# Two transformer blocks on one core: the seams between stages reordered, and memory attention's logits from query parts

## The chip, the cores and the metric

The kernel runs on one core of a Trainium2 chip. The engines are TensorE (PE), which multiplies matrices into PSUM, VectorE (DVE), ScalarE (ACT), GpSimd (POOL) and SyncE (SP), which here only issues transfers. Each engine works its instructions off in the order in which the program gives them. The metric is the device time of one execution in microseconds.

## The reference

Two blocks follow one another on 1024 rows of 1024 channels, all in float32. The first mixes three branches by gates, projects, and runs a gated MLP; the second has spatial gating, attention in a window and attention to 256 memory rows. Cut to what the change touches:

```python
def hybrid_layer(h, ...):
    ...
    y_b = attn @ w_b
    ...
    m = g[:, :, 0] * y_a + g[:, :, 1] * y_b + g[:, :, 2] * y_c
    h = h + m @ w_o
    hn = rms_norm(h, norm2_g)
    gate, up = jnp.split(hn @ w_gate_up, 2, axis=-1)
    return h + (jax.nn.silu(gate) * up) @ w_down

def memory_cross_attention(q, mem_k, mem_v):
    logits = jnp.einsum('bshd,bmhd->bhsm', q, mem_k).astype(jnp.float32) * (dh ** -0.5)
    probs = jax.nn.softmax(logits, axis=-1)
    out = jnp.einsum('bhsm,bmhd->bshd', probs.astype(mem_v.dtype), mem_v)
    return out.reshape(b, s, h * dh)

def second_block(x, mem, ...):
    h = rms_norm_2(x, pre_norm_g)
    a_u, a_v, sq, sk, sv, mq, z = jnp.split(h @ w_in, split_at, axis=-1)
    y_a = chunked_spatial_gating(jax.nn.gelu(a_u), jax.nn.gelu(a_v), ...)
    y_b = sliding_window_attention(sq, sk, sv, sinks, rel_bias)
    mk, mv = jnp.split(rms_norm_2(mem, mem_norm_g) @ w_mem_kv, 2, axis=-1)
    y_c = memory_cross_attention(mq, mk, mv)
    y = jnp.concatenate([y_a, y_b, y_c], axis=-1) * jax.nn.silu(z)
    return x + rms_norm_2(y @ w_out, post_norm_g)
```

Memory attention has 4 heads of 64 channels, so a query of one head fills half of the 128 rows that a product contracts.

## The kernel before

**Products in parts.** A float32 operand is split into a high part, rounded to fp32r, and a low part, the remainder. A product of two float32 matrices is then three fp32r products into one PSUM bank, high by high, high by low, low by high: `mm3`, lines L296 to L298, called from `proj_t` (weights as the stationary operand) and `proj_r` and `rows512` (rows as the stationary operand).

**Weights.** The class `Weights` walks a list (`plan`) of units of 128x1024 elements in the order in which the stages use them. `load_to` issues a unit's transfer on SP (L84) into one of three buffers (wraw), `split_to` makes the high part on ACT (L96) and the low part by a subtraction (L97) on POOL or DVE; the parts (wpart) have eight buffers. `get` hands units to a stage. `ahead_to(i)` splits the units up to i beyond those in use, and alternates between DVE and POOL for the low part; `ahead()` splits two ahead with POOL. Where the program calls them decides behind what these instructions stand in each engine's queue.

**Order.** The order on every engine is that in which the program's text issues the instructions. Stages follow one another: wb (the attention branch and the gated sum m), wo, the memory keys and values (mkv), the MLP (gate and up, then down), z, a (two halves: v with a layer norm, u), spatial gating, the heads' projections (qkv), attention (att2), and the last projection w2. At each seam the first weight units of the next stage must be split while the last tiles of this one are evicted. Side work runs on credits: a `Side` gets so many microseconds by each `tick` in PE's loops, times a rate, and issues its next step when it has credit. In wb two of them run: the normalisation and transposition of the 256 memory rows (`mem_steps`, scale L1090, transposes L1096, copies L1101 and L1102), and the expansion of the window's bias.

**wb.** For each of four weight pairs, two halves of the rows and two column tiles, PE fills a tile; DVE multiplies it by a gate (L1130) and adds the other branches' sum (L1131), both loaded by POOL (L1114 and L1115) one tile ahead; ACT writes the high part mh (L1132), POOL the low part ml (L358).

**wo to MLP.** `add_rows` adds a tile to the residual (L1303), takes the sum of squares and stores the row half (L1227, on SP). `norm2_b` norms a row block. The second half of wo is a loop of its own over the row blocks, with the norms and the splits for mkv between the tiles. `t1_sum`, `t2_sum` and `t3_sum` (L1239, L1566, L1243) form the sums of row blocks for the MLP's products; gate and up are computed with seven products of halves in place of eight. `gu_load`, `gu_sums` and `gu_prep` load, add and split the weights for one of them (L1265, L1272 to L1274, L1297 and L358), and `gu_mm(n, turns)` issues product n with the listed transposes between its matmuls: `turn4`, four transposes on PE (L1207) into a bank called ax, evicted by ACT (L1210) and DVE (L1211).

**rows512.** It fills eight row tiles from four weight units. The last two run unit by unit, and one tile's eviction is held back to behind them; then the next stage's units are split, and the last tiles are evicted by `put`. For the v half of stage a, `put` runs a layer norm by steps on DVE and POOL (L1803, L1804), so that an eviction brings POOL two products that wait for DVE.

**Attention.** Sixteen items, one of the window and one of memory for each row block, go through four stages: logits (L1933, PE; maxima on DVE), exps (ACT), turn (transposes L1969 of the probabilities and their copies), values (L1991). PE's queue interleaves stages of neighbouring items. The memory logits are one fp32 matmul 128x256 a head, whose queries mqp are zero in the other head's 64 rows.

## Time and profile before

| | |
|---|---|
| runs: median (lowest to highest) | 2199.52 us (2195.73 to 2200.37), 3 runs |
| the profiled execution | 2198.24 us |
| its span | 2196.5 us |
| its mean granted clock | 0.992 of full speed |

The span is what the trace covers, from the first instruction to the last; 1.74 us of the execution lie outside. The granted clock is TensorE's, 1.00 for 2.4 GHz and 0.50 for 1.2 GHz. Busy shares of the engines are means over stages that differ much: stages with products keep PE full, and what the other engines do is seen by PE only where it waits for them.

### The profile page before, as it was taken

How to read it: one execution, taken by the hardware profiler on the slowest of the kernel's cores; microseconds unless marked ns; L12 is line 12 of the kernel's file. 1: busy time of each engine (PE TensorE's matmuls, PEld its weight loads, DVE VectorE, ACT ScalarE, POOL GpSimd, SP SyncE). 2: the span in 40 equal slices, each digit the busy share in tenths (PEclk: the TensorE clock that was granted, in tenths of full speed). 3: DMA queues.
4: the chain of work that ended last, by engine and by line, in shares of the span. 5: the costliest groups of instructions: out<-in, count | busy, mean ns of one | idle time of the engine just before them, and what ended most of it. 6: DMA issues, size and time to landing. Idle time of an engine off the chain costs nothing.

```text
span 2196.5 us, 28194 instructions
## 1 busy us (share of the span) xinstructions
PE 2130.6 (97%) x10319; PEld 1796.9 (82%) x10319; DVE 1394.0 (63%) x2720; ACT 776.1 (35%) x1476; POOL 773.4 (35%) x675
## 2 busy tenths in 40 slices
PE   7999999999999999989989999999999999999998
PEld 7788888998888898777777888888788778778986
DVE  7688899889886587642765544454776651822725
ACT  4574211112112676332243333333433342212621
POOL 1213323225452320571048777785300001551201
PEclk9999999999999999999999999999999999999999
DMA  4121122112331000355213434334898422110014
GB/s 150 64 71 63 58 77 97 39 58 77 106 106 39 21 1 10 101 142 176 99 47 103 154 105 139 116 124 143 313 387 298 164 90 86 39 48 30 1 48 154
DMA packets 141227, 227.64 MB, mean 104 GB/s; under 512 B 15148, under 2 KB 77328, under 8 KB 141088
## 3 DMA queue, kind: packets, MB, share of 16 engines
q1 hardware_dynamic: 124544, 181.43, 24.6%
q0 software_dynamic: 9408, 30.15, 4.4%
q10 hardware_dynamic: 7136, 14.25, 1.7%
q8 instruction: 81, 1.33, 0.2%
q14 instruction: 58, 0.48, 0.1%
HBM read 170.46 MB, written 55.31 MB: 103 GB/s over the span
## 4 chain that ended last, share of the span: by engine, by line
PE 81%; DVE 7%; issue 4%; POOL 3%; DMA 3%; ACT 2%; SPq 0%; ACTq 0%; DVEq 0%; POOLq 0%
PE mm L297 23%; PE mm L298 23%; PE mm L296 23%; PE ax L296 2%; PE ax L297 2%; PE ax L298 2%; PE mm L1002 1%; PE ax L1991 1%; PE mm L1933 1%; POOL wpart L97 1%; PE mm L383 1%; DVE scores L611 1%; DMA ev<-mpart 1%; PE mm L1969 1%; DVE rt L287 1%
## 5 line engine op out<-in xcount | busy, mean ns | idle before, releaser
L97 POOL TENSOR_TENSOR wpart<-wraw,wpart 128x1024 fp32r<-128x1024 f32 (+1 forms) x88 | 211.4, 2416 | 726.6 <-ACT wpart L96 726.5
L297 PE MATMUL mm<-xl,wpart 128*128 128x512 f32 (+2 forms) x736 | 269.9, 367 | 0.0
L296 PE MATMUL mm<-xh,wpart 128*128 128x512 f32 (+2 forms) x736 | 268.9, 365 | 0.0
L298 PE MATMUL mm<-xh,wpart 128*128 128x512 f32 (+2 forms) x736 | 268.6, 365 | 0.0
L654 DVE MAX8 m<-scores 128x8 f32<-128x272 f32 (+6 forms) x224 | 188.8, 843 | 6.3 <-POOL scores L616 0.2
L656 DVE MATCH_REPLACE8 scores<-m,scores 128x272 f32<-128x272 f32 (+6 forms) x224 | 184.9, 826 | 0.0
L296 PE MATMUL mm<-tm,wpart 128*128 128x512 f32 x440 | 172.3, 392 | 1.3 <-DVE hb L1386 1.3
L298 PE MATMUL mm<-tm,wpart 128*128 128x512 f32 x440 | 171.4, 390 | 0.0
L297 PE MATMUL mm<-tm,wpart 128*128 128x512 f32 x440 | 171.3, 389 | 0.0
L96 ACT ACTIVATE wpart<-wraw 128x1024 fp32r<-128x1024 f32 (+1 forms) x110 | 112.7, 1049 | 161.2 <-issue 95.2
L358 POOL TENSOR_TENSOR wpart<-hb,wpart 128x512 fp32r<-128x512 f32 x88 | 118.8, 1357 | 135.9 <-ACT wpart L1297 135.9
L296 PEld LDWEIGHTS mm<-xh,wpart 128*128 128x128 f32 x736 | 138.4, 188 | 20.3
L297 PEld LDWEIGHTS mm<-xl,wpart 128*128 128x128 f32 x736 | 138.2, 188 | 19.7
L298 PEld LDWEIGHTS mm<-xh,wpart 128*128 128x128 f32 x736 | 138.5, 188 | 19.1
L297 PE MATMUL mm<-wpart,hh 128*128 128x512 f32 x256 | 101.9, 398 | 6.6 <-POOL wpart L97 3.6
L296 PE MATMUL mm<-wpart,hh 128*128 128x512 f32 x256 | 101.4, 396 | 0.0
L298 PE MATMUL mm<-wpart,hl 128*128 128x512 f32 x256 | 101.3, 396 | 0.0
L97 DVE TENSOR_TENSOR wpart<-wraw,wpart 128x1024 fp32r<-128x1024 f32 (+1 forms) x22 | 28.6, 1309 | 110.4 <-ACT wpart L96 110.3
L296 PEld LDWEIGHTS mm<-tm,wpart 128*128 128x128 f32 x440 | 82.6, 188 | 18.7 <-DVE hb L1386 1.7
L298 PEld LDWEIGHTS mm<-tm,wpart 128*128 128x128 f32 x440 | 82.6, 188 | 17.5 <-POOL wpart L358 0.2
L1297 ACT ACTIVATE wpart<-hb 128x512 fp32r<-128x512 f32 x88 | 55.0, 627 | 117.7 <-DVE hb L1290 60.1
L297 PEld LDWEIGHTS mm<-tm,wpart 128*128 128x128 f32 x440 | 82.7, 188 | 16.7
(388 smaller groups left out, 5393.0 us busy)
## 6 DMA issues: line engine op xcount, KB each, us to landing
wraw<-in_w_in_dram SPq DMA_DIRECT2D x68, 512.0 KB, 3.6
hd<-hb SPq DMA_DIRECT2D x100, 256.0 KB, 2.4
tm<-in_w_down_dram SPq DMA_DIRECT2D x99, 256.0 KB, 5.3
wraw<-in_w_gate_up_dram SPq DMA_DIRECT2D x44, 512.0 KB, 3.7
tm<-hd SPq DMA_DIRECT2D x33, 512.0 KB, 7.2
wraw<-hd SPq DMA_DIRECT2D x33, 256.0 KB, 5.3
mpart<-ev POOLq DMA_DIRECT2D x32, 256.0 KB, 2.3
ev<-mpart POOLq DMA_DIRECT2D x32, 256.0 KB, 3.4
```

The lines of the kernel that those rows point to most:

```text
L96: nc.scalar.activation(hi[:, :nk * w], r, AF.Copy)
L97: (low or nc.gpsimd).tensor_tensor(lo[:, :nk * w], r, hi[:, :nk * w].bitcast(F32), op=ALU.subtract)
L287: nc.vector.scalar_tensor_tensor(t, y, v, y, op0=ALU.mult, op1=ALU.mult)
L296: nc.tensor.matmul(o, sh, mh, start=start, stop=False, skip_group_check=more)
L297: nc.tensor.matmul(o, sh, ml, start=False, stop=False, skip_group_check=more)
L298: nc.tensor.matmul(o, sl, mh, start=False, stop=stop, skip_group_check=more)
L358: (eng or nc.gpsimd).tensor_tensor(out_lo, src, hi.bitcast(F32), op=ALU.subtract)
L383: nc.tensor.transpose(tp[:, k * 128:k * 128 + P], r[:, kk * 128:(kk + 1) * 128], ident[:P, :P])
L611: nc.vector.scalar_tensor_tensor(s, r, c["wr"][:, h:h + 1], s, op0=ALU.mult, op1=ALU.add)
L654: nc.vector.max(m8, s)
L656: nc.vector.match_replace(out=s, in_to_replace=m8, in_values=s, imm_value=TAKEN)
L1297: nc.scalar.activation(hi, src, AF.Copy)
```

## The change

The first part moves instructions at the seams and leaves the arithmetic alone: `rows512` splits the next units before the held eviction; wb's loop splits the last units before the last tile's eviction; the memory side work has a rate of 1.25; the work around the memory keys' products and the MLP's first products is issued in another order, with the transposes one product later; the low parts of z's third and fourth units go to DVE, each behind two row blocks' transposes; spatial gating goes over row halves outside and groups inside. A small tile for the sinks is shared with another.

The second part concerns memory attention. The 128 contracted rows now hold the high part of a head's queries in one half and the low part in the other (mqp, fp32r, by `put_parts`: two half copies on ACT, two subtractions on DVE, two transfers between row halves on POOL's queue, for each of four tiles). The keys stand in both halves, split into mkh and mkl. A head's logits are two fp32r products 128x256, with mkh and with mkl, in place of one fp32 product. The memory queries are projected first among the heads, and the clearing of mqp is dropped.

```diff
@@ -219,6 +219,6 @@
         plan_wide("a", w_in2, 512 * j)
+    plan_cols("s", w_in2, 256 * 6)
     for k0 in (0, 4):
         plan.append(("s", [cols(w_in2, 1024 + 64 * hd, 64, k0) for hd in (0, 2, 1, 3)], 4, 256))
-    for j in (5, 6):
-        plan_cols("s", w_in2, 256 * j)
+    plan_cols("s", w_in2, 256 * 5)
     for j in range(2):
@@ -350,4 +350,4 @@
         W.load_to(W.nu + 4)
-        put(held, order[-3])
         W.ahead_to(nxt)
+        put(held, order[-3])
         put(os_[0], order[-2])
@@ -1105,3 +1105,3 @@
 
-    memside = Side(mem_steps(), 1.1)
+    memside = Side(mem_steps(), 1.25)
     biasside = Side(bias_steps())
@@ -1120,3 +1120,6 @@
         units = W.get("wb", 2)
-        W.ahead()
+        if j < 3:
+            W.ahead()
+        else:
+            W.ahead_to(2)
         for t0, n in HALVES:
@@ -1129,2 +1132,4 @@
                 proj_t(o, units, ct * 128, oh, ol, 0, n)
+                if f == 7 and t0:
+                    W.ahead_to(4)
                 nc.vector.tensor_tensor(g, o, g, op=ALU.mult)
@@ -1133,3 +1138,2 @@
                 lo_of(ml[:, f, t0:t0 + n], p, mh[:, f, t0:t0 + n])
-    W.ahead_to(4)
     close(aop)
@@ -1142,5 +1146,2 @@
         gu_load(0)
-        norm2_b(7)
-        t1_sum(2)
-        t1_sum(3)
         e = ev()
@@ -1156,8 +1157,8 @@
         gu_prep(0, nc.vector)
+        norm2_b(7)
+        t1_sum(2)
+        t1_sum(3)
+        gu_prep(1, nc.vector)
         gu_sums(0)
         gu_load(1)
-        gu_prep(1, nc.vector)
-        for t in range(4):
-            t3_sum(t)
-        gu_prep(2, nc.vector)
         e = ev()
@@ -1171,3 +1172,3 @@
         nc.scalar.dma_start(mkd[1], e)
-        gu_prep(3, nc.vector)
+        gu_prep(2, nc.vector)
 
@@ -1321,2 +1322,4 @@
         proj_r(o, mh, ml, t * 128, wo, 0, 512)
+        if t == 7:
+            W.split_to(W.nu + 2, nc.vector)
         if t:
@@ -1327,4 +1330,2 @@
             t1_sum(t - 5)
-        if t == 7:
-            W.split_to(W.nu + 2, nc.vector)
         add_rows(1)(o, t)
@@ -1571,17 +1572,19 @@
 
-    gu_mm(0, [(5, 0), (5, 1), (5, 2)])
-    gu_prep(4)
+    gu_mm(0)
     gu_out(0)
-    gu_mm(1, [(7, 0), (7, 1), (7, 2)])
-    gu_prep(5)
-    gu_mm(2, [(5, 3), (3, 0), (3, 1)])
+    gu_mm(1, [(5, 0), (5, 1), (5, 2)])
+    for t in range(4):
+        t3_sum(t)
+    gu_prep(3)
+    gu_prep(4)
+    gu_mm(2, [(5, 3), (7, 0), (7, 1)])
     gu_out(2)
-    gu_mm(3, [(7, 3), (3, 2)])
-    for t in range(3):
-        t2_sum(t)
+    gu_prep(5)
+    gu_mm(3, [(7, 2), (7, 3), (3, 0)])
     gu_sums(1)
     gu_prep(6)
-    gu_mm(4, [(3, 3), (6, 0)])
-    t2_sum(3)
     gu_out(1)
+    gu_mm(4, [(3, 1), (3, 2), (3, 3)])
+    for t in range(4):
+        t2_sum(t)
     gu_out(3)
@@ -1589,3 +1592,3 @@
     gu_prep(7)
-    gu_mm(5, [(6, 1), (6, 2)])
+    gu_mm(5, [(6, 0), (6, 1)])
     gu_out(5)
@@ -1594,3 +1597,3 @@
     gu_prep(8)
-    gu_mm(6, [(6, 3), (4, 0)])
+    gu_mm(6, [(6, 2), (6, 3), (4, 0)])
     gu_out(6)
@@ -1736,3 +1739,4 @@
         to_cols(h[:, t, :], hh, hl, t * 128)
-    W.ahead_to(4)
+        if t % 2:
+            W.split_to(W.ns + 1, nc.vector)
 
@@ -1770,3 +1774,3 @@
             "(q j) -> q j", j=383)[:, :256])
-    sink = swp.tile([128, 16], F32, name="sink")[:, :4]
+    sink = cm0[:, :4]
     nc.scalar.dma_start(sink, A["attn_sinks_2"].to_broadcast([128, 4]))
@@ -1841,4 +1845,4 @@
     rows512(W.get("a", 4), h2o, list(range(NT)), u_put)
-    for g in range(4):
-        for n0 in (0, 4):
+    for n0 in (0, 4):
+        for g in range(4):
             o = mm_tile()
@@ -1856,5 +1860,5 @@
     sqp = qkv.tile([128, 4, S], F32, name="sqp")
-    mqp = qkv.tile([128, 4, S], F32, name="mqp")
+
+    mqp = qkv.tile([128, 4, S], F32R, name="mqp")
     nc.gpsimd.memset(sqp, 0.0)
-    nc.gpsimd.memset(mqp, 0.0)
     skT = qkv.tile([128, S], F32, name="skT")
@@ -1863,6 +1867,11 @@
     nc.gpsimd.memset(svr[:, S:], 0.0)
-    mkT = qkv.tile([128, 2, 256], F32, name="mkT")
+    mkr = qkv.tile([128, 4, 256], F32, name="mkr")
+    mkh = qkv.tile([128, 4, 256], F32R, name="mkh")
+    mkl = mkr.bitcast(F32R)
     mv = qkv.tile([128, 2 * 256 + 64], F32, name="mv")
     nc.gpsimd.memset(mv[:, 512:], 0.0)
-    nc.scalar.dma_start(mkT.rearrange("p a k -> p (a k)"), mkd[0])
+    for a in range(2):
+        for r in (0, 64):
+            nc.scalar.dma_start(mkr[r:r + 64, a:4:2, :],
+                                mkd[0, 64 * a:64 * a + 64, :].rearrange("p (b k) -> p b k", b=2))
     nc.scalar.dma_start(mv[:, :512], mkd[1])
@@ -1881,2 +1890,14 @@
 
+    def put_parts(h0, h1):
+        def put(o, t0, n):
+            c = slice(t0, t0 + n)
+            t = ev().bitcast(F32R)
+            nc.scalar.activation(mqp[:64, h0, c], o[:64], AF.Copy)
+            nc.scalar.activation(t[64:], o[64:], AF.Copy)
+            nc.vector.tensor_tensor(t[:64], o[:64], mqp[:64, h0, c].bitcast(F32), op=ALU.subtract)
+            nc.vector.tensor_tensor(mqp[64:, h1, c], o[64:], t[64:].bitcast(F32), op=ALU.subtract)
+            nc.gpsimd.dma_start(mqp[64:, h0, c].bitcast(F32), t[:64].bitcast(F32))
+            nc.gpsimd.dma_start(mqp[:64, h1, c].bitcast(F32), t[64:].bitcast(F32))
+        return put
+
     def put_k(o, t0, n):
@@ -1890,3 +1911,9 @@
     W.ahead()
+    proj_cols(units, 0, put_parts(0, 1))
+    proj_cols(units, 128, put_parts(2, 3))
+    units = W.get("s", 2)
+    W.ahead()
     proj_cols(units, 0, put_heads(sqp, 0, 2))
+    nc.scalar.activation(mkh, mkr, AF.Copy)
+    lo_of(mkl, mkr, mkh, nc.vector)
     proj_cols(units, 128, put_heads(sqp, 1, 3))
@@ -1895,6 +1922,5 @@
     proj_cols(units, 128, put_v)
-    proj_cols(units, 0, put_k)
-    units = W.get("s", 2)
-    W.ahead()
-    proj_cols(units, 0, put_heads(mqp, 0, 1))
+    o = mm_tile()
+    proj_t(o, units, 0, hh, hl, 0, 512)
+    put_k(o, 0, 512)
     for a in range(2):
@@ -1904,3 +1930,5 @@
         nc.vector.tensor_copy(svr[:, a * 512:a * 512 + 512], tp)
-    proj_cols(units, 128, put_heads(mqp, 2, 3))
+    o = mm_tile()
+    proj_t(o, units, 0, hh, hl, 512, 512)
+    put_k(o, 512, 512)
     close(h2p)
@@ -1931,5 +1959,10 @@
                 hd = 2 * b + a
-                keys = skT[:, k0:k0 + w] if kind == "swa" else mkT[:, b, :]
-                nc.tensor.matmul(o[:, a, :w], qp[:, hd, i * 128:i * 128 + 128], keys, start=True,
-                                 stop=True, skip_group_check=True)
+                qs_ = qp[:, hd, i * 128:i * 128 + 128]
+                if kind == "swa":
+                    nc.tensor.matmul(o[:, a, :w], qs_, skT[:, k0:k0 + w], start=True,
+                                     stop=True, skip_group_check=True)
+                    continue
+                for c, keys in enumerate((mkh, mkl)):
+                    nc.tensor.matmul(o[:, a, :], qs_, keys[:, hd, :], start=c == 0, stop=c == 1,
+                                     skip_group_check=True)
             if kind == "swa":
```

On ACT at the end of wb: `mh<-ev` is an eviction's high part, `wpart<-wraw` a weight unit's, `mth` the memory rows' transposes, `junk,ss<-mrow` their sum of squares, `ssq` wo's. Before:

```order
L1101 ACTIVATE mth<-mm,vcols 128x128 x8
L1132 ACTIVATE mh<-ev 128x512 x2
L362 ACTIVATE junk,ss<-mrow 128x1024
L1132 ACTIVATE mh<-ev 128x512 x2
L96 ACTIVATE wpart<-wraw 128x1024 x2
L1132 ACTIVATE mh<-ev 128x512
L1101 ACTIVATE mth<-mm,vcols 128x128 x8
L1132 ACTIVATE mh<-ev 128x512 x3
L96 ACTIVATE wpart<-wraw 128x1024 x2
L362 ACTIVATE junk,ssq<-hb 128x512 x5
```

and now:

```order
L96 ACTIVATE wpart<-wraw 128x1024 x2
L1137 ACTIVATE mh<-ev 128x512
L362 ACTIVATE junk,ss<-mrow 128x1024
L1137 ACTIVATE mh<-ev 128x512 x2
L1101 ACTIVATE mth<-mm,vcols 128x128 x4
L1137 ACTIVATE mh<-ev 128x512
L96 ACTIVATE wpart<-wraw 128x1024 x2
L1101 ACTIVATE mth<-mm,vcols 128x128 x4
L1137 ACTIVATE mh<-ev 128x512 x3
L96 ACTIVATE wpart<-wraw 128x1024 x2
L1137 ACTIVATE mh<-ev 128x512
L362 ACTIVATE junk,ssq<-hb 128x512 x5
```

The second pair of wo's units stood behind the sixteenth eviction and stands behind the fifteenth; the sum of squares of the second memory block and the copies of its transposes stand earlier among the evictions, the latter in two groups.

On DVE from the last norm of wo to the MLP's first products: L1239/L1240 and L1243/L1244 are the sums t1 and t3, `hb<-wraw` the weight sums, L358 low parts of the MLP's weights, `tm<-ax` evictions of transposes, L1566 the sum t2. Before:

```order
L375 SCALAR_TENSOR_TENSOR hb<-hb,ry,ev 128x512 x2
L1239 TENSOR_TENSOR hb<-hb 128x512 x2
L358 TENSOR_TENSOR wpart<-wraw,wpart 128x512
L1272 TENSOR_TENSOR hb<-wraw 128x512
L1273 TENSOR_TENSOR hb<-hb,wraw 128x512
L1274 TENSOR_TENSOR hb<-wraw 128x512
L358 TENSOR_TENSOR wpart<-wraw,wpart 128x512
L1243 TENSOR_TENSOR hb<-hb 128x512 x4
L358 TENSOR_TENSOR wpart<-wraw,wpart 128x512 x2
L1211 TENSOR_TENSOR tm<-ax,tm 128x4x128 x11
L1566 TENSOR_TENSOR hb<-hb 128x512 x3
L1272 TENSOR_TENSOR hb<-wraw 128x512
```

and now:

```order
L375 SCALAR_TENSOR_TENSOR hb<-hb,ry,ev 128x512 x2
L1240 TENSOR_TENSOR hb<-hb 128x512 x2
L358 TENSOR_TENSOR wpart<-wraw,wpart 128x512
L1273 TENSOR_TENSOR hb<-wraw 128x512
L1274 TENSOR_TENSOR hb<-hb,wraw 128x512
L1275 TENSOR_TENSOR hb<-wraw 128x512
L358 TENSOR_TENSOR wpart<-wraw,wpart 128x512
L1212 TENSOR_TENSOR tm<-ax,tm 128x4x128 x3
L1244 TENSOR_TENSOR hb<-hb 128x512 x4
L1212 TENSOR_TENSOR tm<-ax,tm 128x4x128 x6
L1273 TENSOR_TENSOR hb<-wraw 128x512
L1274 TENSOR_TENSOR hb<-hb,wraw 128x512
```

The first three evictions of transposes stand ahead of the four t3 sums, which were ahead of all eleven, and the two splits behind those sums have moved away.

On PE in attention: skT and sqp are keys and queries of the window, mkT, mkh and mkr keys of memory (mkr's tile holds mkl, the low part), mqp their queries, `ident,P` the transposes of probabilities, svr and mv the values. One item of memory and its neighbours, before:

```order
L1933 MATMUL mm<-skT,sqp 128x256 x4
L1991 MATMUL ax<-svr,pt 128x128 x4
L1969 MATMUL mm<-ident,P 128x128 x8
L1933 MATMUL mm<-mkT,mqp 128x256 x4
L1991 MATMUL ax<-mv,pt 128x128 x8
```

and now:

```order
L1962 MATMUL mm<-skT,sqp 128x256 x4
L2024 MATMUL ax<-svr,pt 128x128 x4
L2002 MATMUL mm<-ident,P 128x128 x8
L1966 MATMUL mm<-mkh,mqp 128x256
L1966 MATMUL mm<-mkr,mqp 128x256
L1966 MATMUL mm<-mkh,mqp 128x256
L1966 MATMUL mm<-mkr,mqp 128x256
L1966 MATMUL mm<-mkh,mqp 128x256
L1966 MATMUL mm<-mkr,mqp 128x256
L1966 MATMUL mm<-mkh,mqp 128x256
L1966 MATMUL mm<-mkr,mqp 128x256
```

Four fp32 matmuls of an item have become eight fp32r ones at the same place.

## Rows read from the trace of the kernel before

**Rows 1.** The page's first section: busy time, share of the span, instructions.
```profile
PE 2130.6 (97%) x10319; PEld 1796.9 (82%) x10319; DVE 1394.0 (63%) x2720; ACT 776.1 (35%) x1476; POOL 773.4 (35%) x675
```

**Rows 2.** PE's waits; columns: in total, times, longest (us).
```profile
PE mm L296 <- ACT wpart L96: 10.4, 2, 8.8
PE mm L297 <- DVE wpart L97: 4.8, 4, 2.9
PE ax L1207 <- DVE tm L1211: 4.5, 2, 4.3
PE mm L297 <- POOL wpart L97: 3.6, 1, 3.6
...
PE mm L298 <- DVE wpart L97: 2.4, 1, 2.4
...
PE mm L296 <- DVE Y L1848: 1.9, 1, 1.9
...
PE mm L1096 <- DVE mrow L1090: 1.6, 1, 1.6
```

**Rows 3.** Table by stretch: us, busy (x) per engine, granted clock, DMA, GB/s.
```profile
991.20:995.80 4.60, 3.91 (x8) 2.76 (x9) 1.42 (x1) 0.89 (x1) 3.98 (x4) 0.50 0.36 72
1094.90:1098.20 3.30, 2.88 (x13) 2.88 (x14) 2.95 (x13) 1.26 (x2) 0.00 (x0) 0.50 0.70 228
1108.60:1115.20 6.60, 5.91 (x19) 4.31 (x18) 1.65 (x3) 2.31 (x4) 1.26 (x1) 0.50 0.00 0
1764.00:1770.60 6.60, 5.88 (x14) 4.67 (x15) 5.10 (x16) 2.46 (x5) 0.00 (x0) 0.50 0.51 178
1907.30:1910.60 3.30, 3.22 (x8) 2.55 (x9) 2.85 (x12) 0.00 (x0) 1.25 (x2) 0.50 0.53 158
```

**Rows 4.** The chain in stage a at full clock: start, us, what.
```profile
1859.95 0.23 PE mm L298
...
1860.63 0.23 PE mm L298
```

**Rows 5.** Timelines of ACT and POOL, end of wb: start, us, what, idle before.
```profile
989.56 0.63 ACT L1132 ACTIVATE mh<-ev 128x512 fp32r<-128x512 f32 x1 [3.36 <-DVE ev L1131]
990.10 1.99 ACT L96 ACTIVATE wpart<-wraw 128x1024 fp32r<-128x1024 f32 x2
...
968.74 4.73 POOL L97 TENSOR_TENSOR wpart<-wraw,wpart 128x1024 fp32r<-128x1024 f32 x2
```

**Rows 6.** Timelines of DVE and POOL, start of z.
```profile
1761.41 3.26 DVE L97 TENSOR_TENSOR wpart<-wraw,wpart 128x1024 fp32r<-128x1024 f32 x1
...
1761.23 2.35 POOL L97 TENSOR_TENSOR wpart<-wraw,wpart 128x1024 fp32r<-128x1024 f32 x1 [195.08 <-ACT wpart L96]
```

**Rows 7.** Timelines of DVE, SP and ACT, end of wo.
```profile
1083.95 2.35 DVE L97 TENSOR_TENSOR wpart<-wraw,wpart 128x1024 fp32r<-128x1024 f32 x2
...
1087.35 0.39 SPq L84 DMA_DIRECT2D wraw<-in_w_mem_kv_dram  x1
...
1092.95 1.06 ACT L96 ACTIVATE wpart<-wraw 128x1024 fp32r<-128x1024 f32 x1 [3.31 <-DMA wraw<-in_w_mem_kv_dram]
```

**Rows 8.** Timeline of ACT in wb.
```profile
929.01 1.04 ACT L362 ACTIVATE junk<-mrow 128x1024 bf16<-128x1024 f32 x1
```

**Rows 9.** Timeline of DVE, start of the MLP.
```profile
1107.59 1.28 DVE L1211 TENSOR_TENSOR tm<-ax,tm 128x512 fp32r<-128x512 f32 x2
```

**Rows 10.** Timeline of POOL between the two halves of a.
```profile
1904.98 2.34 POOL L97 TENSOR_TENSOR wpart<-wraw,wpart 128x1024 fp32r<-128x1024 f32 x1
```

**Rows 11.** The chain in attention.
```profile
2048.96 1.73 PE mm L1933 x8
```

**Rows 12.** Table by stretch: memory keys' products, and attention.
```profile
1084.00:1092.00 8.00, 6.77 (x56) 6.74 (x56) 5.42 (x7) 2.64 (x5) 0.00 (x0) 1.00 0.50 161
2045.00:2075.00 30.00, 30.00 (x226) 28.52 (x226) 23.02 (x74) 19.33 (x68) 5.00 (x7) 1.00 0.00 1
```

**Rows 13.** The page's DMA issues: count, KB each, us to landing.
```profile
hd<-hb SPq DMA_DIRECT2D x100, 256.0 KB, 2.4
```

More of the change, by code (lines that the diff above doesn't have):

```diff
@@ L350, in rows512 @@
         W.load_to(W.nu + 4)
+        W.ahead_to(nxt)
         put(held, order[-3])
-        W.ahead_to(nxt)
         put(os_[0], order[-2])
@@ L1570, in t4_sum @@
         nc.gpsimd.tensor_tensor(ht[t, 1], ht[t, 1], ht[t + 4, 1], op=ALU.subtract)
-    gu_mm(0, [(5, 0), (5, 1), (5, 2)])
+    gu_mm(0)
+    gu_out(0)
+    gu_mm(1, [(5, 0), (5, 1), (5, 2)])
+    for t in range(4):
+        t3_sum(t)
+    gu_prep(3)
     gu_prep(4)
-    gu_out(0)
-    gu_mm(1, [(7, 0), (7, 1), (7, 2)])
+    gu_mm(2, [(5, 3), (7, 0), (7, 1)])
+    gu_out(2)
     gu_prep(5)
-    gu_mm(2, [(5, 3), (3, 0), (3, 1)])
-    gu_out(2)
-    gu_mm(3, [(7, 3), (3, 2)])
-    for t in range(3):
-        t2_sum(t)
+    gu_mm(3, [(7, 2), (7, 3), (3, 0)])
     gu_sums(1)
     gu_prep(6)
-    gu_mm(4, [(3, 3), (6, 0)])
-    t2_sum(3)
     gu_out(1)
+    gu_mm(4, [(3, 1), (3, 2), (3, 3)])
+    for t in range(4):
+        t2_sum(t)
     gu_out(3)
```

## The prediction

> **What bounds the kernel now.** The page's first section says that TensorE (PE) is busy 97% of the span [rows 1], so only two things can shorten it: less matmul time, or fewer stretches in which PE stands still or runs at its lower clock. Second I read the list of PE's waits: what the diff touches is a handful of single long waits, each at a seam between two stages, with the engine that ended it named [rows 2]. Third, the table by stretch right behind those waits: the granted clock is 0.50 there, 1.2 instead of 2.4 GHz, five times [rows 3]. Busy time at half the clock is twice what it would be, so those five cost half of their PE busy time: 3.91, 2.88, 5.91, 5.88 and 3.22 us give 2.0, 1.4, 3.0, 2.9 and 1.6 us, 10.9 together. [...] Fourth, the timelines of the engine that PE waits for. The three matmuls of a product take 0.68 us of the chain at full clock (1859.95 to 1860.63), 0.227 each [rows 4]; this is the price of a place in PE's queue.
>
> **The change part by part.**
>
> *wb to wo.* PE waits 8.8 us for the high part of wo's third weight unit. ScalarE (ACT) makes it at 990.10, right behind the last eviction of mh at 989.56 [rows 5]. Evictions come 3.99 us apart there (3.36 waiting and 0.63 work), held by transfers, so the data of the weights lie ready and only the place in ACT's queue is late. After the change the two copies stand behind the fifteenth eviction, one step (4 us) sooner. The ladder itself moves sooner too: the two weight subtractions of 4.73 us on GpSimd (POOL) [rows 5], which hold up POOL's issue of the next tiles' transfers, become one, and the eight small copies for memory rows move up. I take 4 to 5 us for this, so that unit 2's high part comes at about 982 instead of 991.1, and PE is there at 982.3 (991.1 less 8.8). Its low part on VectorE (DVE), 1.2 us long, then makes PE wait about 0.6, and unit 3's low part on POOL, half of 4.73 long, about 2.2. Today it waits 8.8 and about 0.7 (one of the four on DVE that make 4.8 [rows 2]), so the gain is 6.7; half of the slow stretch, 1.0, goes too. 7.7 in all. Ends: 3 if only the step in the queue counts and the low parts are late, 11.5 if all wait and slow clock go.
>
> What speaks against it is what the trace shows of two engines at once: at 1761.41 one such subtraction on DVE took 3.26 us beside the same on POOL (2.35) [rows 6], where two alone took 2.35 [rows 7], 1.2 each. With 3.3 in place of 1.2 the low part is 2.1 later and the gain 5.6. The Trainium skill ("SBUF — State Buffer", Who interferes with whom) says that a DVE instruction with two SBUF inputs contends with a GpSimd instruction that reads SBUF, and the one that came first keeps the port for its whole length; the two rows agree. By that page the low parts moved to DVE here, where POOL subtracts for ml, may each be stretched, and the sum would be 2 us worse.
>
> *Memory rows' transposes.* Side work is handed out by credits, now 1.25 instead of 1.1 a us, so the transposes L1096 stand 24 matmuls (5.5 us) and at the second row block 39 (8.9 us) sooner in PE's queue. PE waits 1.6 at the first today [rows 2], for a scale whose sum of squares ran on ACT at 929.01 [rows 8]. In the new order that sum stands before the fifth eviction instead of behind it, about 8 us sooner, and its chain before the fifth pair's. So the wait stays near 1.2 and none is added: no term. If the scale didn't move, the waits would be 7.1 (5.5 and 1.6) and 8.9 us.
>
> *wo to MLP.* Three things. The subtractions of the memory weights on DVE stood behind a norm and start 2.5 us sooner (before: 1083.95, 2.35 for the two [rows 7]): of the 2.4 us wait 0.3 is left, a gain of 2.1. But that norm and the last addition of wo come 1.2 later, and behind its stores in SP's queue stands the load of the memory weights' fourth unit (1087.35), for which ACT waited until 1092.95 [rows 7]. The load so goes out 1.2 later, while PE is there 2.1 sooner: the waits of 1.6 on ACT (10.4 less 8.8) and about 0.9 on DVE [rows 2] grow by 3.3, and with them the slow stretch by about 0.7. Loss 4.0. The MLP's first product no longer has transposes between its matmuls, and their evictions on DVE come ahead of four subtractions and two splits instead of behind them. The wait of 4.3 (DVE got to them at 1107.59 [rows 9]) goes, and half of the 3.0 of slow clock behind it: 5.8. Next late is a product's wait for the eviction of the bank that it adds to, as today. Sum 3.9 gained; ends: 9 gained (no loss at the fourth unit), 2 lost (the wait goes to a new place of the MLP's start).
>
> *down to z.* The wait of 2.9 is for the subtraction of 3.26 us. Its two low parts now both go to DVE, between the evictions; POOL has none. At 1.2 instead of 3.26 it ends 2 us sooner, and its wait falls to about 1.1; of the slow 2.9 I take 1.8 off. The transposes ahead of it wait as today. Gain 3.6 (ends 1 and 6).
>
> *a to a, and spatial gating.* The low part of the fourth unit stands on POOL behind two products of the layer norm that wait for DVE, and starts at 1904.98 [rows 10]. In the new order both low parts stand together ahead of these, so it is ready at about 1902, before PE needs it at 1903.7: the wait of 3.6 and the slow 1.6 go, 5.2 (ends 2 and 5.2). The gating now takes the first four row blocks for all groups first; the 1.9 us wait for Y, the product of the last blocks, has four tiles' work ahead of it: 1.9 gained (ends 0 and 1.9).
>
> *Attention's memory logits.* One fp32 product set of an item takes 1.73 us on PE [rows 11]. Now it is eight fp32r products 128x256; such products ran at 6.77 us for 56, 0.121 each [rows 12]: 0.97 an item. Eight items: 8 x 0.76 = 6.1. In this stage PE is busy 30.00 of 30 us, DVE 23.02 and ACT 19.33 [rows 12], so the next engine has a fifth left, and the gain is real. Those 56 products had 56 weight loads, busy 6.74 us, beside them; if loads and products didn't overlap here, an item would take 8 x 0.24, 1.93, a loss of 0.2. Ends: 1.6 lost and 7 gained; I take the overlapped price, since the row with it has the same shapes. The Trainium skill ("TensorE: Matmul & The Clock Gate", LDWEIGHTS) puts a load at its columns divided by 1.2, 107 ns for 128; as an estimate by that page, load and product one behind the other take 0.21 to 0.23, 1.7 to 1.8 an item, and the change would give nothing here. The trace's two equal busy times in one stretch speak against it.
>
> What the parts of the queries cost: eight more half copies on ACT and eight subtractions on DVE (under 0.7 us each by the 128x512 ones at 989.56 [rows 5] and 1107.59 [rows 9]), one copy and one subtraction of keys (about 1.2 each, as a weight unit's), all beside some twelve tiles of 24 matmuls, 5.4 us each. The eight DMAs of 128 KB land after a time bounded by 2.4 us (256 KB [rows 13]); the memory queries come first of the heads now, some 40 us before they are used. Nothing, while this cover stands; without it, 8 x 2 x 0.7 = 11 us and a DMA's 2.4.
>
> **Sum.** 7.7 + 3.9 + 3.6 + 5.2 + 1.9 + 6.1 = 28.4 us. The profiled execution took 2198.24 us, 1.74 more than its span, and becomes 2169.8; the median of the runs is 1.28 above it: 2171.
>
> **The rivals.**
> *B: the seams re-form.* A wait goes, and another of 2 us or more stands a few matmuls later, with its slow stretch: wo's unit 3, the memory weights' fourth unit, z's third. For it speaks that five seams in a row have the same form, and DVE stretched beside POOL; against it, that each new place has been followed above. Half of the seams' 22.3 us is lost, 11: 2182.
> *C: the logits give nothing*, because loads and products don't overlap, or because DVE and the exps on ACT, which stand between an item's logits and its transposes, become the bound. For: every item is a chain through three engines; against: 23 of 30 us. 2177.
> *D, the other side:* the credits move the transposes L1096 ahead of their data, and the scale's chain is held by the eviction ladder, one step of 4 us later than it stands today. PE then waits 7.1 + 4 and 8.9 + 4, 24 us, 22.4 more than now, with some 2.3 of slow clock behind each as at the other seams, and the ladder behind it, late by as much, gives back wb to wo's 7.7: 2171 + 22.4 + 4.6 + 7.7 = 2206. It decides from 22 us of waits at these two places on. Against: the order has the chain sooner too.
> *E: the seams stay as they are*, the waits being set by transfers and not by places in queues (the ladder's 3.36 a step, the load on SP), and the logits alone come: 2199.5 less 6 is 2193.5.
>
> **How the numbers follow.** Forecast 0.55, B 0.22, C 0.10, D 0.06, E 0.07. Its own range is 2163 to 2179, by the ends of wb to wo, wo to MLP and the logits. To hold eight in ten the range goes from 2162 to 2189, which takes in B and C; D and E are left out with part of the forecast's own tails. 0.2% is 4.4 us, about what a measurement here can tell: E is faster by more than that in most of its cases. Faster 0.91, the same 0.04, slower 0.05.
>
> **What would show it.** In the profile after: PE's waits no longer list 8.8 (ACT, wo), 4.3 (ax, DVE), 3.6 (POOL) and 1.9 (Y); the wait for the memory weights' fourth unit stands at 4 to 6 us in place of 2.4; the wait at L1096 under 2; eight rows of mkh/mkr products of about 0.97 an item; PE busy in attention still full. It is wrong if PE's busy time falls by less than 10 us (6.1 of logits and 7.8 of slow clock are 13 or so), if a wait over 3 us stands at a place that had none, or if L1096 waits over 5.

## The result, and the profile after

The changed kernel takes 2181.57 us (median of 4 runs, 2180.65 to 2181.99) against 2199.29 us (4 runs, 2195.73 to 2200.37): a ratio of 0.9923, with a 95% interval from 0.9908 to 0.9938. That is 17.7 us less, where 28.4 were forecast. The profiled execution took 2181.52 us, with a span of 2179.8.

The lengths of the stages show where this comes from; each is counted from the stage's first matmul to that of the next, in us, in the two profiled executions. The down stage (217.3 and 217.1) and the last projection (99.6 and 99.5) are left out.

| stage | before | after | difference | forecast |
|---|---|---|---|---|
| wb | 91.6 | 95.7 | +4.1 | |
| wo | 102.8 | 99.5 | -3.4 | with wb: -7.7 |
| memory keys and values | 18.6 | 17.8 | -0.8 | |
| MLP to down | 440.3 | 442.8 | +2.5 | with the line above: -3.9 |
| z and a | 189.7 | 179.2 | -10.5 | -8.8 |
| spatial gating | 7.6 | 5.4 | -2.2 | -1.9 |
| heads' projections | 66.2 | 66.2 | 0.0 | 0 |
| attention | 74.9 | 68.7 | -6.1 | -6.1 |

Everything behind the first block came as forecast or better, 19 us with the rest. The first block, where 11.6 us were to be gained, lost 2.4. The page's first section and PE's waits (in total, times, longest) of the changed kernel, against [rows 1, 2]:

```profile
PE 2120.6 (97%) x10319; PEld 1789.7 (82%) x10319; DVE 1404.1 (64%) x2726; ACT 780.0 (36%) x1481; POOL 772.9 (35%) x681
```

```profile
PE ax L1208 <- DVE tm L1212: 6.7, 4, 2.1
PE mm L297 <- DVE wpart L97: 6.5, 3, 4.9
PE mm L296 <- ACT wpart L96: 3.7, 2, 2.1
PE mm L1096 <- DVE mrow L1090: 2.7, 2, 1.8
...
PE mm L298 <- DVE wpart L97: 0.8, 1, 0.8
...
PE ax L1208 <- DVE hb L1567: 0.7, 1, 0.7
PE ax L1208 <- DVE hb L1244: 0.7, 1, 0.7
```

The wait of 8.8 for wo's third unit is gone from ACT's line, and 4.9 of it stands in DVE's. The waits of 3.6 on POOL and 1.9 on Y are gone, and of the 2.9 at z 0.7 is left. The evictions of transposes (L1208, L1212; L1207 and L1211 before) cost 6.7 in four waits, and the sums that the transposes read 1.4 in two, where they cost 4.5 in two. PE's busy time fell by 10.0, 6.1 of it the logits' products.

In attention, the chain and the table by stretch (us, busy and count of PE, PEld, DVE, ACT, POOL, granted clock, DMA, GB/s) answer to [rows 11, 12]:

```profile
2036.03 0.95 PE mm L1966 x8
```

```profile
2033.00:2063.00 30.00, 30.00 (x248) 29.18 (x247) 24.45 (x81) 20.15 (x67) 5.33 (x8) 1.00 0.01 2
```

Eight products take 0.95 us where the fp32 ones took 1.73, PE is still never idle, and DVE is at 24.45 of 30: no other engine became the bound.

The timelines of DVE and POOL at z and between the halves of a answer to [rows 6, 10]:

```profile
1761.16 1.22 DVE L97 TENSOR_TENSOR wpart<-wraw,wpart 128x1024 fp32r<-128x1024 f32 x1
...
1764.69 1.22 DVE L97 TENSOR_TENSOR wpart<-wraw,wpart 128x1024 fp32r<-128x1024 f32 x1
...
1896.97 2.40 POOL L97 TENSOR_TENSOR wpart<-wraw,wpart 128x1024 fp32r<-128x1024 f32 x1 [3.04 <-ACT wpart L96]
```

Each subtraction on DVE takes 1.22 now that none runs on POOL beside it, and POOL's is done at 1899.4; neither wait is left but 0.7 at z. The two slow stretches that stood behind these waits [rows 3] are gone.

Now the seam that failed, wb to wo, on ACT, DVE and POOL (start, us, engine, line, what; in brackets what ended the idle time before):

```profile
986.45 0.63 ACT L1137 ACTIVATE mh<-ev 128x512 fp32r<-128x512 f32 x1 [3.48 <-DVE ev L1136]
986.99 1.99 ACT L96 ACTIVATE wpart<-wraw 128x1024 fp32r<-128x1024 f32 x2
...
988.06 5.38 DVE L97 TENSOR_TENSOR wpart<-wraw,wpart 128x1024 fp32r<-128x1024 f32 x1 [1.64 <-ACT wpart L96]
...
988.26 1.28 POOL L358 TENSOR_TENSOR ml<-ev,mh 128x512 fp32r<-128x512 f32 x1
...
990.00 2.35 POOL L97 TENSOR_TENSOR wpart<-wraw,wpart 128x1024 fp32r<-128x1024 f32 x1
```

The high parts' copies stand behind the fifteenth eviction, as planned, but that eviction is at 986.45, not at about 981 as the forecast had it: the ladder (the evictions, one behind the other) didn't come sooner. And DVE's subtraction takes 5.38 us: it ends at 993.44, 1.09 behind the second of POOL's two pieces (1.28 and 2.35). The trace before had such a price already, in wb, where a DVE addition that takes 0.69 elsewhere stood beside three subtractions on POOL, ml's (1.30) and the two here:

```profile
921.61 6.83 DVE L1131 TENSOR_TENSOR ev<-ev 128x512 f32<-128x512 f32 x1
...
923.13 4.75 POOL L97 TENSOR_TENSOR wpart<-wraw,wpart 128x1024 fp32r<-128x1024 f32 x2
```

At the start of the MLP the sums t3 (L1244) and t2 (L1567) run into the same:

```profile
1109.40 4.67 DVE L1244 TENSOR_TENSOR hb<-hb 128x512 f32<-128x512 f32 x4
1114.00 1.28 DVE L1212 TENSOR_TENSOR tm<-ax,tm 128x512 fp32r<-128x512 f32 x2
...
1129.76 4.68 DVE L1567 TENSOR_TENSOR hb<-hb 128x512 f32<-128x512 f32 x4
...
1109.36 1.28 POOL L358 TENSOR_TENSOR wpart<-wraw,wpart 128x512 fp32r<-128x512 f32 x1 [69.72 <-ACT wpart L1298]
1110.60 1.73 POOL L358 TENSOR_TENSOR wpart<-hb,wpart 128x512 fp32r<-128x512 f32 x1
```

The four t3 sums take 4.67 us, 2.49 before, with POOL's two low parts beside them, and the next evictions of transposes come at 1114.00 behind them. The four t2 sums take 4.68. Last, the table by stretch where the clock is low in the changed kernel, from wb to the MLP, against [rows 3]:

```profile
888.30:891.30 3.00, 2.85 (x7) 2.16 (x7) 3.00 (x6) 3.00 (x7) 0.00 (x0) 0.50 0.03 3
932.70:935.40 2.70, 2.70 (x10) 2.20 (x9) 1.39 (x2) 0.21 (x1) 0.49 (x1) 0.50 0.41 152
994.10:997.00 2.90, 2.90 (x8) 2.30 (x7) 0.67 (x1) 0.63 (x1) 1.49 (x2) 0.50 0.48 165
1094.10:1096.40 2.30, 2.30 (x12) 2.06 (x10) 1.11 (x1) 1.80 (x4) 0.00 (x0) 0.50 0.90 292
1116.90:1119.80 2.90, 2.90 (x9) 2.33 (x10) 0.00 (x0) 0.94 (x2) 1.28 (x1) 0.51 0.02 6
```

Two of these five stand in wb, where the kernel before had none; at half the clock they cost half of their busy time, 1.4 each. Not every wait has such a stretch behind it: the kernel before waited 2.4 us among the memory keys' products [rows 2] and ran on at full clock [rows 12].

### The profile page after: what moved, and what is told of

Same layout as the page of the kernel before. It is cut to its first block, busy times and chain, and to the rows that moved or that the text cites. A ratio compares the mean times of both kernels' runs of the same rounds, so it can differ in the third digit from the quotient of the medians.

```text
span 2179.8 us, 28244 instructions
## 1 busy us (share of the span) xinstructions
PE 2120.6 (97%) x10319; PEld 1789.7 (82%) x10319; DVE 1404.1 (64%) x2726; ACT 780.0 (36%) x1481; POOL 772.9 (35%) x681
## 4 chain that ended last, share of the span: by engine, by line
PE 82%; DVE 7%; issue 4%; POOL 2%; DMA 2%; ACT 2%; ACTq 0%; DVEq 0%; SPq 0%; POOLq 0%
PE mm L297 23%; PE mm L298 23%; PE mm L296 23%; PE ax L296 2%; PE ax L298 2%; PE ax L297 2%; PE mm L1002 1%; PE ax L2024 1%; PE mm L383 1%; DVE wpart L97 1%; DVE scores L611 1%; DMA ev<-mpart 1%; PE mm L2002 1%; PE mm L1962 1%; DVE ev L1136 1%
## 5 line engine op out<-in xcount | busy, mean ns | idle before, releaser
L358 POOL TENSOR_TENSOR wpart<-hb,wpart 128x512 fp32r<-128x512 f32 x88 | 119.4, 1363 | 64.4 <-ACT wpart L1298 64.4
L358 POOL TENSOR_TENSOR wpart<-wraw,wpart 128x512 fp32r<-128x512 f32 x63 | 85.5, 1365 | 79.4 <-ACT wpart L1298 79.4
L97 DVE TENSOR_TENSOR wpart<-wraw,wpart 128x1024 fp32r<-128x1024 f32 (+1 forms) x24 | 34.4, 1440 | 106.8 <-ACT wpart L96 106.7
L298 PE MATMUL mm<-wpart,hl 128*128 128x512 f32 x256 | 99.6, 389 | 0.0
```

The source lines that it names most:

```text
L97: (low or nc.gpsimd).tensor_tensor(lo[:, :nk * w], r, hi[:, :nk * w].bitcast(F32), op=ALU.subtract)
L298: nc.tensor.matmul(o, sl, mh, start=False, stop=stop, skip_group_check=more)
L358: (eng or nc.gpsimd).tensor_tensor(out_lo, src, hi.bitcast(F32), op=ALU.subtract)
```

## The experiments

Theory A says: the gain stems from the stages behind the first block, and the first block's seams gave back what they gained, because DVE's subtractions are stretched by POOL's and because the evictions' ladder sets when wo can go on. Its rival, theory B (not the prediction's rival B), says: stages are coupled through the clock, and the sum isn't made of parts.

**e1: the logits alone, on the kernel before.** The edit is shown against the kernel before, cut to the products.

```diff
-                nc.tensor.matmul(o[:, a, :w], qp[:, hd, i * 128:i * 128 + 128], keys, start=True,
-                                 stop=True, skip_group_check=True)
+                for c, keys in enumerate((mkh, mkl)):
+                    nc.tensor.matmul(o[:, a, :], qs_, keys[:, hd, :], start=c == 0, stop=c == 1,
+                                     skip_group_check=True)
...
```

> Only the second part of the change on the kernel before: memory queries in parts, keys in both halves, two fp32r products a head, the heads' new order; all seams as before. Theory A (the gain of the whole change comes from the stages behind the first block, the first block's seams gave back what they gained): attention takes 6.1 us less, as in the changed kernel, nothing else moves, 2193. Theory B (the stages are coupled by the clock, and what a stage gains depends on what stood before it): the gain here is under 3 or over 9 us.

2192.71 us, ratio 0.9972 (0.9962 to 0.9981) to the kernel before, which took 2199.70 here. Attention took 68.7 us, as in the changed kernel. Not all else stood still: z and a took 187.9 in place of 189.7, without the slow stretch behind z's wait, though this seam wasn't edited, and the heads' projections 67.9 in place of 66.2, with a slow stretch at their start. By 1 to 2 us a stage theory B has a point.

**e2: everything from the end of down on, and rows512.** The edit is against the changed kernel.

```diff
-    memside = Side(mem_steps(), 1.25)
+    memside = Side(mem_steps(), 1.1)
...
-    gu_mm(0)
-    gu_out(0)
-    gu_mm(1, [(5, 0), (5, 1), (5, 2)])
+    gu_mm(0, [(5, 0), (5, 1), (5, 2)])
...
```

> All edits from the end of the down stage on (z's low parts, rows512, spatial gating, queries and logits), the first block's text from wb to the MLP as before, but for rows512 in wo's first half. Theory A: from z on the same 19 us as in the changed kernel, the first block as before, so about 2180, 1 to 3 us less than the changed kernel. Theory B: wb's two new slow stretches or others of the kind come here too, and it stands at 2183 or above.

2180.20 us, ratio 0.9916 (0.9901 to 0.9931), which is no worse than the whole change. PE's waits have the old seam and the new end:

```profile
PE mm L296 <- ACT wpart L96: 8.9, 1, 8.9
PE ax L1207 <- DVE tm L1211: 4.9, 2, 4.7
```

**e3: the first block's edits alone.** The edit is against the kernel before.

```diff
-    memside = Side(mem_steps(), 1.1)
+    memside = Side(mem_steps(), 1.25)
...
+                if f == 7 and t0:
+                    W.ahead_to(4)
...
+    for t in range(4):
+        t3_sum(t)
...
```

> Only the edits of the first block (side work's rate, wb's splits, order around the memory keys and the MLP's first products), all else as before. Theory A: no gain, 2199 to 2203: the wait for wo's third unit is again about 1.5 and then 4.9, the one for the transposes' evictions is replaced by several of 0.7 to 2.1. By the prediction's terms it would be 2188.

2202.10 us, ratio 1.0008 (0.9998 to 1.0018): no gain. Its waits:

```profile
PE mm L297 <- DVE wpart L97: 8.7, 3, 4.9
PE ax L1208 <- DVE tm L1212: 6.8, 4, 2.1
...
PE mm L297 <- POOL wpart L97: 3.6, 1, 3.6
```

The two halves of the change add up: in medians, 19.5 less and 2.4 more make 17.1 less, and the whole has 17.7; in spans, 18.9 less and 3.4 more make 15.5 less, and the whole has 16.8. That the first block's edits gave nothing by themselves is shown; what undid them is the subject of the next ones. e4 to e10 are single runs, read by stage; their edits are against the changed kernel, which took 2180.65 to 2181.99.

**e4: both low parts of wo's last units on DVE.**

```diff
-                    W.ahead_to(4)
+                    W.split_to(W.nu + 4, nc.vector)
```

> The changed kernel, with the low parts of wo's third and fourth unit both on DVE, none on POOL. If the subtraction of 5.4 us on DVE was long because POOL subtracted beside it (1.3 for ml and 2.35 for the fourth unit), it has only the 1.3 beside it now and takes 2.5 at most, both are done 4.5 us after the first began, PE's wait of 4.9 is 2 or less, and wo ends about 3 us sooner. If it was long for another reason (the transfers that run there), it stays over 4 us and the second comes behind it: the wait stays at 4.9 and another of 1 us or more follows.

```profile
988.08 3.71 DVE L97 TENSOR_TENSOR wpart<-wraw,wpart 128x1024 fp32r<-128x1024 f32 x2 [1.64 <-ACT wpart L96]
...
988.28 1.28 POOL L358 TENSOR_TENSOR ml<-ev,mh 128x512 fp32r<-128x512 f32 x1
```

The first subtraction takes 2.58, beside POOL's ml piece (1.28), the second 1.21, 3.71 together, where one took 5.38. PE's longest wait on DVE fell from 4.9 to 2.1, and wo's end came 2.1 us sooner. The subtraction was long because POOL subtracted. In all it is 2180.79 us, 0.8 less: the memory keys and values took 1.5 longer.

**e5: the memory rows' rate back at 1.1.**

```diff
-    memside = Side(mem_steps(), 1.25)
+    memside = Side(mem_steps(), 1.1)
```

> The changed kernel with the memory side work's rate back at 1.1. Theory A: wb took 4.1 us longer in the changed kernel, 1.1 of it by the waits at the memory rows' transposes (1.8 and 0.9 in place of 1.65) and the rest by two slow stretches, one of them behind the first of these waits, the other at wb's start, which the rate can't touch. So wb is 1 to 3 us shorter than in the changed kernel, and the waits here are 1.65 and under 0.8. Rival (the ladder of evictions is what the rate made later): wo's third unit's high part comes 3 us or more sooner than 987.0 to 988.0. If the rate did good, as the prediction's word on it was, nothing gets better.

2181.6 us, no difference. wb is 3.2 us shorter, but wo's third unit isn't ready sooner, so that PE waits for it instead (PE's timeline):

```profile
987.07 0.79 PE L296 MATMUL mm<-wpart,mh 128*128 128x512 f32 x1 [3.74 <-ACT wpart L96]
992.49 0.80 PE L297 MATMUL mm<-wpart,mh 128*128 128x512 f32 x1 [4.62 <-DVE wpart L97]
```

The ladder, not PE, sets when wo can go on: wb ended at 980.5 here, 983.6 in the changed kernel and 979.5 before, and the fifteenth eviction stood at 985.4, 986.5 and 985.6. The rival fell: without the higher rate the ladder is 1.0 us sooner and not 3. It waits in its turn for transfers, here ahead of the fifteenth:

```profile
984.72 0.69 DVE L1136 TENSOR_TENSOR ev<-ev 128x512 f32<-128x512 f32 x1 [2.81 <-DMA ev<-mpart]
```

Both slow stretches of wb are missing, that at its start too, though nothing ahead of it differs and the wait ahead of it is 1.50 in both (here, from 888.30, at full clock):

```profile
888.30:891.30 3.00, 2.78 (x12) 2.16 (x12) 3.00 (x6) 3.00 (x7) 0.00 (x0) 1.00 0.03 3
```

The same stretch is slow in some of the kernels that were run (the changed one, e2, e3, e7, e9) and not in the others, before and e11 among these. It isn't the change's doing, and what decides it stays open. The other one comes with the rate: a slow stretch behind a wait at the memory rows' transposes stands in all nine kernels with the rate 1.25 and in none of the four with 1.1 (before, e1, e2 and this one). wb takes 91.6 to 92.9 us in these four and 95.5 to 97.3 in the nine. Five of the nine start wb at full clock and take 95.5 to 95.8, no less than the changed kernel's 95.7: PE comes to the transposes sooner and waits 3.1 to 3.2 us there in place of 1.8. So the rate costs wb some 3 us, which the changed kernel would have spent at wo's third unit anyway.

**e6: the sums of the MLP in two groups.**

```diff
+    for t in range(3):
+        t3_sum(t)
     gu_mm(1, [(5, 0), (5, 1), (5, 2)])
-    for t in range(4):
-        t3_sum(t)
+    t3_sum(3)
...
+    t2_sum(0)
     gu_mm(4, [(3, 1), (3, 2), (3, 3)])
-    for t in range(4):
+    for t in range(1, 4):
         t2_sum(t)
```

> The changed kernel with three of the four t3 sums ahead of the MLP's second product's transposes, where DVE stands idle for 1.2 us, and one behind it, and with the first t2 sum one product sooner. If the new waits at the MLP's start (0.7, 2.1, 0.7, 1.3 and 1.3 us) come from evictions queued behind four sums in a row, they come to 3 us or less together and the MLP's section is 2 to 3 us shorter. If they are what the two banks for transposes cost in any order, they stay at 6 in sum.

```profile
1103.70 1.89 DVE L1244 TENSOR_TENSOR hb<-hb 128x512 f32<-128x512 f32 x3
...
1108.18 1.78 DVE L1244 TENSOR_TENSOR hb<-hb 128x512 f32<-128x512 f32 x1
```

```profile
PE ax L1208 <- DVE tm L1212: 2.5, 2, 2.1
```

2174.25 us, 7.3 less (e5 and e8, run on the same chip, took 2181.60 and 2181.66). The three sums without POOL beside them take 0.63 each, the one with it 1.78. The waits at L1208 fell from 6.7 (and two of 0.7 for the sums themselves) to 2.5. This is more than the 2 to 3 us expected: the MLP is 6.1 us shorter, the rest is in the stages before it, which the edit doesn't touch. Evictions queued behind sums were the loss at the MLP's start; what the t3 and the t2 sums gave each wasn't separated.

**e7: the MLP's two low parts on DVE.**

```diff
-    gu_prep(3)
-    gu_prep(4)
+    gu_prep(3, nc.vector)
+    gu_prep(4, nc.vector)
```

> The changed kernel with the low parts of the MLP's fourth and fifth operand on DVE in place of POOL, behind the t3 sums. If the four sums took 4.67 us instead of 2.49 because POOL subtracted beside them, they take 2.5 here, and with the two low parts (0.7 each) DVE is free 0.8 us sooner for the evictions: PE's wait of 2.1 falls to 1.3 or so. If the sums are slow for another reason they stay at 4.7 and the wait grows to 3.4.

```profile
1111.52 2.49 DVE L1244 TENSOR_TENSOR hb<-hb 128x512 f32<-128x512 f32 x4
```

The four sums take 2.49 us with nothing on POOL, 4.67 with it: the stretching is shown. The wait stayed at 2.0, since the low parts now stand ahead of the evictions. The MLP is 0.9 us shorter, but the stages ahead of it, which the edit doesn't touch, came out 2.1 longer: 2183.52 us, nothing gained.

**e8: the fourth unit's load ahead of wo's last store.**

```diff
             W.split_to(W.nu + 2, nc.vector)
+            W.load_to(W.nu + 4)
```

> The changed kernel, the memory weights' fourth unit's load issued ahead of wo's last store instead of behind it. By the trace its buffer is free at about 1084.3 and its load went out at 1089.9, behind that store. If SP's queue is what holds it, the load goes out by 1086, ACT's copy doesn't wait for it, and the waits of 2.1 and 0.9 at the fourth unit go, with part of a slow stretch: 3 to 4 us less. Rival: ACT's and DVE's own queues (evictions, a norm) hold the unit anyway, and under 1 us is gained.

```profile
1083.31 0.38 SPq L84 DMA_DIRECT2D wraw<-in_w_mem_kv_dram  x1
...
1088.54 0.63 ACT L362 ACTIVATE junk<-hb 128x512 bf16<-128x512 f32 x1 [5.57 <-DVE hb L1304]
...
1090.12 2.00 ACT L96 ACTIVATE wpart<-wraw 128x1024 fp32r<-128x1024 f32 x2
```

The load went out 6.6 us sooner and gained nothing (2181.66 us): ACT does the last two units' copies at 1090.12, behind a sum of squares (1088.54) that waits for DVE's norm and addition. PE's waits of 2.1 and 0.9 are still there; by their place, the first product of the memory values, they are the third unit's and not the fourth's, as the expectation had it. The rival was right.

**e9: wo's split one eviction sooner.**

```diff
-                if f == 7 and t0:
-                    W.ahead_to(4)
+                if f == 6 and t0:
+                    W.split_to(W.nu + 4, nc.vector)
```

> The changed kernel, wo's third and fourth unit split one eviction sooner (ahead of the fifteenth tile's), both low parts on DVE. Theory: what holds them is their place behind an eviction of the ladder, which itself didn't move, and the subtraction on POOL beside DVE's. Behind the fourteenth eviction (982.3) the copies run from 982.9 as PE frees their buffers, the low parts are done by 987, and PE, there at 986.5, waits 1 us at most in place of 1.6 and 4.9; wo to the memory keys is 5 to 7 us shorter. Rival: the copies wait for PE to free the buffers of wb's last units until 983.4 and the ladder behind them grows, so that the gain is under 3 or comes back as a wait in wo's fifth to eighth row block.

```profile
983.04 0.63 ACT L1137 ACTIVATE mh<-ev 128x512 fp32r<-128x512 f32 x1 [3.29 <-DVE ev L1136]
983.58 1.04 ACT L96 ACTIVATE wpart<-wraw 128x1024 fp32r<-128x1024 f32 x1
985.03 1.06 ACT L96 ACTIVATE wpart<-wraw 128x1024 fp32r<-128x1024 f32 x1 [0.41 <-issue]
...
984.65 3.25 DVE L97 TENSOR_TENSOR wpart<-wraw,wpart 128x1024 fp32r<-128x1024 f32 x2 [1.65 <-ACT wpart L96]
```

2176.05 us. The copies run at 983.58 and 985.03, and both waits at wo are gone; wo takes 90.6 us, 8.8 less than in the changed kernel, of which 6.5 are the waits and most of the rest the slow stretch behind them. The fifteenth eviction comes 2.8 later for it, and nobody waits. The edit also has both low parts on DVE; e4 did this alone and wo took 97.1, so the other 6.5 are the place's. That confirms the place behind the ladder as the cause. wb and the MLP took 1.2 longer each, with slow stretches that fell otherwise, so that 5.5 us of the 8.8 are left in all.

**e10: the memory weights' third unit sooner as well.**

```diff
-            W.split_to(W.nu + 2, nc.vector)
+            W.split_to(W.nu + 3, nc.vector)
+            W.load_to(W.nu + 4)
```

> The changed kernel, the memory weights' third unit split with the first two, ahead of the norm and the last addition, and the fourth's load ahead of the last store. The load alone gained nothing at this wait, since ACT reaches the third unit's copy only behind the last sum of squares, which waits for the norm and the addition on DVE. Theory: with the third unit's copy ahead of these the wait of 2.1 goes, and 0.6 or less is left at the fourth unit; the section to the MLP is 2 to 3 us shorter. Rival: the buffers of the parts are freed too late by wo, and the copy only moves the wait to the norm, the addition and the first evictions of the MLP, nothing gained.

```profile
1092.80 0.42 PE L296 MATMUL mm<-wpart,mth 128*128 128x256 f32 x1 [1.82 <-ACT wpart L96]
```

2182.18 us: the third unit's wait of 2.1 is gone, and 1.8 stands at the fourth, whose copy is still behind the same sum of squares. The rival was right: the wait has only moved.

**e11: e6, e9 and e10 together.**

```diff
-                if f == 7 and t0:
-                    W.ahead_to(4)
+                if f == 6 and t0:
+                    W.split_to(W.nu + 4, nc.vector)
...
-            W.split_to(W.nu + 2, nc.vector)
+            W.split_to(W.nu + 3, nc.vector)
+            W.load_to(W.nu + 4)
...
+    for t in range(3):
+        t3_sum(t)
     gu_mm(1, [(5, 0), (5, 1), (5, 2)])
-    for t in range(4):
-        t3_sum(t)
+    t3_sum(3)
...
```

> The changed kernel with the three together: wo's units one eviction sooner with low parts on DVE, the memory weights' third unit sooner, and the t3 and t2 sums in two groups each, which alone gave 7.3 us. Theory, each seam being its own queue: 7.3, 5 to 7 and 2 to 3 add up, 2165 to 2168. Rival, a seam's gain is given back at the next one: 2172 or more.

2166.04 us (5 runs, 2165.97 to 2168.22), ratio 0.9849 (0.9836 to 0.9863): better than both kernels. The span is 15.5 us under the changed kernel's; e6 and e9 alone were 7.3 and 5.8. By stage, wo is 8.8 shorter, as in e9, the MLP 5.8 (6.1 in e6) and the memory keys and values 1.1. The gains of the seams add up, as the theory had it, but the expected sum also held 2 to 3 us for e10's edit, which alone gave none; that the time lies within it is in part luck. The rate is still 1.25 here, and PE waits 3.2 us at the first of the memory rows' transposes; e11 with the rate 1.1 was not tried.

```profile
PE 2116.0 (98%) x10319; PEld 1787.5 (83%) x10319; DVE 1399.2 (65%) x2727; ACT 780.3 (36%) x1481; POOL 771.2 (36%) x680
```

## Why the prediction was right, and where not

The time lies in the range, 10.6 us above the forecast and 2.6 above the forecast's own range; it is covered because the range had been widened to take in rivals B and C. Rival B's time, 2182, is the one that came, and its mechanism too, but not spread over the seams: all of it in the first block, while the others gave 2 us more than forecast. One of the prediction's own signs of being wrong came: a wait over 3 us (4.9, wo's third unit) where 0.7 had stood. PE's busy time fell by 10.0, just at the limit set for it; the 7.8 us of slow clock named beside that limit don't follow from the sum, whose terms hold 5.2 (1.0, 1.5, 1.8 and 1.6, less 0.7).

- *Logits*: right in size and mechanism, 6.1 forecast and measured; e1 shows it by itself. Weight loads overlapped, rival C fell.
- *Spatial gating, a, z*: right. The sum of 10.7 became 12.7, since both slow stretches went entirely and z's wait fell to 0.7 instead of 1.1; the step that moved the low parts to DVE had this size because POOL had nothing there (1.22).
- *wb to wo*: wrong, 7.7 forecast, 0.7 lost. The failed sentence is "the ladder itself moves sooner too [...] I take 4 to 5 us for this". The step in ACT's queue gave 3.1 us (988.08 for 991.19; 4.1 in e5), the ladder gave none (fifteenth eviction at 986.45, 985.57 before), since its steps wait for transfers and the memory rows' copies now stand elsewhere in it, not less. The second failure is the price of the low part: 1.2 was taken with 3.3 as the bad end, and it was 5.38, outside both, so that the wait for it grew from 0.7 to 4.9 and ate what the step gave. The row for the bad end [rows 6] had one POOL instruction beside DVE's, the place here had two; a row with three, 6.83 us at 921.61, was in the trace and wasn't used.
- *The Trainium skill's rule* ("SBUF — State Buffer", Who interferes with whom) was weighed and priced at 2 us worse; it was the right warning and cost 4.2. In one point the trace differs from the page: the one that comes first is to keep the port, but DVE's started at 988.06, POOL's at 988.26, and POOL's took its usual 1.28 and 2.35 us while DVE's took 5.38. Here the measurement decides: it was DVE that was stretched. Where DVE's had begun a whole microsecond ahead (991.17, POOL's at 992.16, in the kernel before), they took 1.45 and 2.68, as the page has it.
- *Memory rows' transposes*: "no term" was wrong by the 3 us or so that the rate costs wb (e5): 1.65 became 1.8 and 0.9 with a slow stretch behind the first, and 3.1 to 3.2 and 0.8 to 1.0 where wb started at full clock. The failed step is that the scale's chain comes as much sooner as its sum of squares. The sum did come 8.2 us sooner (920.80 for 929.01), but the scale only 3.8 (930.58 for 934.37), and PE's place moved by 5.5. One small instruction of the chain, 0.2 to 0.4 us elsewhere, stood beside three subtractions on POOL, ml's and the two here:

```profile
922.53 5.65 DVE L287 SCALAR_TENSOR_TENSOR rt<-ry,rv 128x1 f32<-128x1 f32 x1
...
923.42 4.73 POOL L97 TENSOR_TENSOR wpart<-wraw,wpart 128x1024 fp32r<-128x1024 f32 x2
```

The loss is hidden in the changed kernel's time, since wo's third unit was late anyway. Rival D, 24 us of waits, fell.
- *wo to MLP*: wrong, 3.9 gained forecast, 1.7 lost. "Their evictions on DVE come ahead of four subtractions [...] instead of behind them" was true of three of eleven. The next ones stood behind the sums, stretched to 4.67 by POOL, and a second set behind t2. I counted the wait that went and didn't follow the evictions of the next two products; e6 shows what that was worth, some 6 us. The loss of 4.0 at the memory weights was over-sized (the waits went from 4.9 to 3.8 in all, and from the fourth unit to the third): it was laid on the load in SP's queue, and e8 shows that ACT's queue holds it.
- *What stays open*: why the stretch at wb's start is slow in some executions and not in others, and what e11 would take with the rate at 1.1.

## What to carry to other kernels

A weight split that stands behind an eviction in an engine's queue inherits the eviction's pace, so moving it by one place pays by no more than that pace: find the last eviction that PE doesn't need and put the split ahead of it. Moving work from POOL to DVE pays where POOL then has nothing with SBUF inputs beside it (1.2 us) and cost 4 us where it had (5.4); look in the trace before for the longest DVE instruction beside POOL's, not for a typical one. It hits small instructions too, and chains through them (5.65 for one of 0.2). When a wait goes, follow the same queue to the next two users of it before counting the gain.
